# Two of the four weight sums of a seven-product step are formed during the up projection and kept in DRAM

## The chip, the core and the metric

The kernel runs on one core of a Trainium2 chip. TensorE (PE in the profile) multiplies, with its weight loads shown apart as PEld; VectorE is DVE, ScalarE is ACT, GpSimd is POOL, and SyncE (SP) only issues transfers. POOL and ACT can issue transfers too. The metric is device time of one execution in microseconds, as a median of several; lower is better.

## The reference

A decoder layer on 272 positions (16 learned meta tokens and 256 tokens) of width 2048, all in float32:

```
u = rmsnorm(h);  proj = u @ w_in            # retention and mLSTM heads
h = h + concat(ret, hm) @ w_out
u = rmsnorm(h, norm_ffn)
up = causal_dwconv(u @ w_up)                # 2048 -> 2 x 5632, three taps
gate, val = split(up)
h = h + (silu(gate) * val) @ w_down         # 5632 -> 2048
return rmsnorm(h)[16:]
```

The change lies in the last product, with `w_down`, and in the up projection ahead of it.

## The kernel before

**Number format.** Each float32 operand is split into a high part, `hi` (a rounded copy, by ACT, line 128 or 707), and a low part, `lo` (the rest, a subtraction by DVE, line 130 or 709). A product then takes three matmuls: high by high, low by high and high by low. So each 128 x 1024 tile of weights costs one transfer, one ACT cast, one DVE subtraction and its matmuls. Weights arrive in `wraw` (4 buffers) by SP; `whi` and `wlo` have 5 buffers each.

**Up projection.** The 44 blocks of 128 hidden channels are handled in two halves of 22. A block takes two projections (gate and value), each of two half tiles of 24 matmuls on 258 columns (lines 137 to 140). Then `conv3` (line 624) scales the result out of PSUM into `cu` (line 626), applies the taps (lines 628 to 630), and `gt = silu(gt) * vt` (line 721) is the activation. In blocks 2 to 17, DVE also transposes a piece of the residual into `hn` (line 622).

**Down projection.** After each half, the 22 blocks make 11 steps `q` of two blocks, and the 2048 output columns make two pairs `b` = 0 and 2 of two blocks of 512 columns. For a step and a pair there are two forms. A *plain* step loads two weight tiles (`load_step`, line 840) and makes 24 matmuls of 512 columns. A *fast* step (`seven`, line 765) sees step and pair as a 2 x 2 by 2 x 2 block product and makes it by the Strassen-Winograd form with seven products, 21 matmuls. It needs sums of activations (POOL, lines 735 to 738, on the way in the up projection) and four sums of weights: line 773 loads all four weight blocks of the step in one transfer of 1024 KB into `raw`, one of two buffers in dead space of `hT`; DVE forms `ta` (two sums in one operation on 1024 elements, line 776) and `tb` (two dependent sums of 512, lines 777 and 778); then four groups are split into `hi` and `lo` and multiplied. Six steps, `FAST = [1, 2, 4, 5, 7, 8]`, are fast. In the last pair of the second half the last of them, `BOTH`, is made plain, so there are 6 + 6 + 6 + 5 = 23 fast steps.

The four products that serve several outputs are put together in `share` (line 813) after the last fast step of a pair: ACT copies one, DVE makes three sums (lines 819 to 824), and POOL adds four tiles `x` onto `hn` by accumulating transfers (`onto`, line 809). The direct sums `cs` follow at the pair's end.

**The end.** In the last pair the last four plain steps leave out the second column block (`alone`). These products come last: first for rows 0 to 127 (`cs[0, 1]`), then for rows 128 to 255 in two halves of 256 columns. DVE adds them onto `hn` (`add`, line 827), ACT squares and sums (`squares`, line 638), and `finish` (line 652) normalises and stores each row block.

**What sets the order.** A scheduler orders each engine's instructions when the kernel is built, from its own estimate of times; `issue_after` adds an ordering and `high_priority` moves code up. On the chip each engine works in its order and waits on semaphores. SP's and POOL's transfers, too, are issued in order.

## Time and profile before

| | |
|---|---|
| median of 3 executions | 1216.38 us (1215.95, 1216.38, 1219.0) |
| the profiled execution's own time | 1215.93 us |
| its span in the trace | 1214.2 us |
| matmul records | 8965 |
| granted TensorE clock | 0.998 |
| DVE busy | 950.8 us (78%) |
| ACT busy | 704.2 us (58%) |
| POOL busy | 131.0 us (11%) |
| moved by DMA | 236.25 MB, mean 195 GB/s |

The span is the time between the first and the last event in the trace; the execution's own time holds 1.7 us more. Matmuls are pipelined, so a matmul's recorded duration is longer than the distance from its start to the next one's, and it is that distance that counts. An engine's idle time is put down to what ended it. By the trace the up projection of the first half runs from about 470 to 718 us, its down projection to about 835, the second half's up projection to about 1087 and its down projection to the end.

### The profile page before, as it was taken

The numbers are of one execution on the slowest core, as the hardware profiler recorded it, in microseconds if no ns is written. First come the engines' busy times: TensorE is split into PE (matmuls) and PEld (weight loads), VectorE is DVE, ScalarE is ACT, GpSimd is POOL, SyncE is SP. The second block draws the span as 40 slices with busy tenths as digits, with TensorE's granted clock in tenths as the row PEclk, the third lists the DMA queues.
The fourth block names the chain that finished last, engine by engine and source line by source line (L and its number), as shares of the span: only waits on it lengthen the run. The fifth ranks groups of instructions, "written<-read, shape, count | busy, mean of one in ns | idle before, by whom it ended". The sixth has DMA issues, their size and how long they took to land.

```text
span 1214.2 us, 22554 instructions
## 1 busy us (share of the span) xinstructions
PE 1203.5 (99%) x8965; PEld 1156.7 (95%) x8965; DVE 950.8 (78%) x1399; ACT 704.2 (58%) x954; POOL 131.0 (11%) x143
## 2 busy tenths in 40 slices
PE   9999999999999999999999999999999999999997
PEld 9999999999999999999999998888999999998885
DVE  8877778766765767788888789896777777789896
ACT  8647746656556556555555556665555555556564
POOL 0100001111010210010101000202020101100232
PEclk9999999999999999999999999999999999999999
DMA  7764555655564655555555634959655555535946
GB/s 277 267 218 157 167 191 169 201 170 187 183 190 140 208 180 180 182 189 180 186 175 189 247 119 170 263 218 315 229 177 189 177 188 177 188 118 195 274 167 184
DMA packets 74010, 236.25 MB, mean 195 GB/s; under 512 B 13488, under 2 KB 17712, under 8 KB 70832
## 3 DMA queue, kind: packets, MB, share of 16 engines
q1 hardware_dynamic: 68640, 223.85, 55.0%
q0 software_dynamic: 4688, 10.10, 4.1%
q8 instruction: 70, 1.15, 0.4%
q10 hardware_dynamic: 576, 0.85, 0.2%
q14 instruction: 36, 0.29, 0.1%
HBM read 222.98 MB, written 4.46 MB: 187 GB/s over the span
## 4 chain that ended last, share of the span: by engine, by line
PE 96%; DVE 1%; DMA 1%; issue 0%; ACT 0%; SPq 0%; POOL 0%; DVEq 0%; ACTq 0%
PE mmps L137 25%; PE mmps L140 25%; PE mmps L138 25%; PE atps L760 3%; PE atps L761 3%; PE atps L763 3%; PE mmps L795 2%; PE mmps L793 2%; PE mmps L792 2%; PE atps L792 1%; PE atps L795 1%; PE atps L793 1%; PE atps L379 1%; DMA hn<-x 0%; DVE wlo L709 0%; PE atps L371 0%
## 5 line engine op out<-in xcount | busy, mean ns | idle before, releaser
L128 ACT CAST whi<-wraw 128x1024 fp32r<-128x1024 f32 x358 | 375.4, 1050 | 357.9 <-PE mmps L138 250.9
L130 DVE TENSOR_TENSOR wlo<-wraw,whi 128x1024 fp32r<-128x1024 f32 x358 | 441.9, 1237 | 81.3 <-ACT whi L128 74.2
L138 PE MATMUL mmps<-ul,whi 128*128 128x258 f32 x1408 | 345.8, 283 | 0.0
L137 PE MATMUL mmps<-uh,whi 128*128 128x258 f32 x1408 | 345.5, 282 | 0.0
L137 PEld LDWEIGHTS mmps<-uh,whi 128*128 128x128 f32 x1408 | 266.1, 189 | 0.1
L138 PEld LDWEIGHTS mmps<-ul,whi 128*128 128x128 f32 x1408 | 265.1, 188 | 0.1
L137 PE MATMUL mmps<-xh,whi 128*128 128x272 f32 (+2 forms) x864 | 220.1, 287 | 0.0
L138 PE MATMUL mmps<-xl,whi 128*128 128x272 f32 (+2 forms) x864 | 218.8, 286 | 0.0
L140 PE MATMUL mmps<-uh,wlo 128*128 128x258 f32 x1408 | 198.9, 284 | 0.0
L140 PEld LDWEIGHTS mmps<-uh,wlo 128*128 128x128 f32 x1408 | 182.4, 189 | 0.0
L137 PEld LDWEIGHTS mmps<-xh,whi 128*128 128x128 f32 x864 | 162.9, 189 | 0.1
L138 PEld LDWEIGHTS mmps<-xl,whi 128*128 128x128 f32 x864 | 162.5, 188 | 0.0
L140 PE MATMUL mmps<-xh,wlo 128*128 128x272 f32 (+2 forms) x864 | 127.1, 286 | 0.0
L140 PEld LDWEIGHTS mmps<-xh,wlo 128*128 128x128 f32 x864 | 114.7, 188 | 0.0
L626 DVE TENSOR_TENSOR cu<-mmps,rstd 128x258 f32<-128x258 f32 x88 | 37.5, 426 | 78.8 <-PE mmps L140 78.5
L707 ACT CAST whi<-wraw 128x1024 fp32r<-128x1024 f32 x46 | 47.7, 1052 | 37.7 <-DVE wraw L778 22.1
L760 PE MATMUL atps<-whi,mh 128*128 128x512 f32 (+1 forms) x166 | 64.0, 387 | 0.0
L761 PE MATMUL atps<-whi,ml 128*128 128x512 f32 (+1 forms) x166 | 63.8, 386 | 0.0
L138 PE MATMUL mmps<-mixl,whi 128*128 128x258 f32 x256 | 63.1, 283 | 0.0
L137 PE MATMUL mmps<-mixh,whi 128*128 128x258 f32 x256 | 62.5, 283 | 0.0
L709 DVE TENSOR_TENSOR wlo<-wraw,whi 128x1024 fp32r<-128x1024 f32 x46 | 56.5, 1244 | 5.5 <-PE mmps L795 3.0
L707 ACT CAST whi<-hT 128x1024 fp32r<-128x1024 f32 (+1 forms) x46 | 37.4, 836 | 20.6 <-PE atps L793 7.7
(267 smaller groups left out, 1620.2 us busy)
## 6 DMA issues: line engine op xcount, KB each, us to landing
wraw<-in_wu SPq DMA_DIRECT2D x176, 512.0 KB, 3.5
wraw<-in_wi SPq DMA_DIRECT2D x108, 512.0 KB, 4.0
hT<-in_wd SPq DMA_DIRECT2D x23, 1024.0 KB, 5.3
wraw<-in_wd SPq DMA_DIRECT2D x42, 512.0 KB, 5.2
wraw<-in_wo SPq DMA_DIRECT2D x32, 512.0 KB, 3.6
hn<-x POOLq DMA_DIRECT2D x28, 256.0 KB, 6.3
wraw<-in_w SPq DMA_DIRECT2D x7, 320.0 KB, 5.1
hT<-in_xT SPq DMA_DIRECT2D x7, 272.0 KB, 5.5
```

The source lines that it names most:

```text
L128: nc.scalar.copy(hi, raw)
L130: nc.vector.tensor_tensor(out=lo, in0=raw, in1=hi.bitcast(F32), op=ALU.subtract)
L137: nc.tensor.matmul(ps, hi[:, k, :], xh(kk), start=kk == first, stop=False)
L138: nc.tensor.matmul(ps, hi[:, k, :], xl(kk), start=False, stop=False)
L140: nc.tensor.matmul(ps, lo[:, k, :], xh(kk), start=False, stop=kk == last)
L626: nc.vector.tensor_tensor(out=u, in0=ps[:, :NQ], in1=rstd2, op=ALU.mult)
L707: copied = nc.scalar.copy(hi, x)
L709: return copied, nc.vector.tensor_tensor(out=lo, in0=x, in1=hi.bitcast(F32), op=ALU.subtract)
L760: nc.tensor.matmul(ps, ah[i], hi[:, i, cols], start=first and i == 0, stop=False)
L761: nc.tensor.matmul(ps, al[i], hi[:, i, cols], start=False, stop=False)
L763: nc.tensor.matmul(ps, ah[i], lo[:, i, cols], start=False, stop=last and i == 1)
L792: nc.tensor.matmul(o, sh[:, f, m, :], hi[:, i, :], start=begin, stop=False)
```

## The change

A fast step's sums S1 and S3 (the former `ta`) no longer stand in the step. For each fast step and pair, an `Early` object loads three of the four weight blocks (768 KB) during the up projection through POOL's queue, DVE subtracts on 1024 elements, and POOL stores the two sums (512 KB) in DRAM as `kept`. The load is held back by `pace`, a POOL addition of one column of the newest activation `gt`. In the first half twelve of the 14 use one buffer, `x4[:, 1:4]`, one every three projections, and the last two the buffers in `hT`; in the second half 12 take turns in three buffers.

In the down projection a fast step makes three loads by SP instead of one: 512 KB into `wraw`, 512 KB of `kept`, and 256 KB of the remaining block, 1280 KB in all. DVE makes two sums of 512 elements there, into the single buffer `t24`, where it made one of 1024 and two of 512.

Seven steps, `[1, 2, 3, 5, 6, 7, 8]`, are fast; two of them, 7 and 8, are plain in the last pair. That makes 7 + 7 + 7 + 5 = 26 fast steps. The last pair's order is `[0, 1, 4, 2, 7, 3, 5, 6, 8, 9, 10]`, so three half steps follow its `share` where two did. Its `share` is moved up by `high_priority`, and one of its four sums is added by DVE instead of by a transfer. Some constants move into a pool that is given back after attention, `ssq` moves into `hn`, and four `x` tiles become one tile `x4`.

```diff
-    ones = consts.tile([P, P], F32, name="ones")
+    ones = pa.tile([P, P], F32, name="ones")
...
-    ssq = up.tile([P, NQ], F32, name="ssq")
+    ssq = hn[:, 0, 0:NQ]
...
+    x4 = midp.tile([P, 4, 512], F32, name="x4")
...
-    FAST = [1, 2, 4, 5, 7, 8]
+    FAST = [1, 2, 3, 5, 6, 7, 8]
...
+    class Early:
+        def __init__(self, b, q, buf):
+            self.buf = buf
+            self.kept = dram.tile([P, 2, 512], F32, name=f"kept{b}_{q % NQD}", bufs=1)
+            nc.gpsimd.dma_start(buf, io["wd7"][b // 2, q][:, 0:3, :])
+        def finish(self):
+            v = self.buf[:, 1:3, :]
+            nc.vector.tensor_tensor(out=v, in0=v, in1=self.buf[:, 0:1, :].to_broadcast([P, 2, 512]), op=ALU.subtract)
+            nc.gpsimd.dma_start(self.kept, v)
...
+        if half == 0:
+            begins = [2 + 3 * i for i in range(12)] + [37, 38, 40, 41][: len(units) - 12]
+        else:
+            begins = [2 + 39 * i // (len(units) - 1) for i in range(len(units))]
...
+                if running:
+                    running.pop().finish()
+                if 2 * jj + s in begins:
...
+                    reached = gt and nc.gpsimd.tensor_tensor(out=pace, in0=gt[:, 0:1], in1=gt[:, 0:1], op=ALU.add)
+                    with tc.issue_after(reached.ins) if gt else nullcontext():
+                        running.append(Early(b, half * NQD + q, homes[n]))
...
-            nc.sync.dma_start(raw, io["wd7"][b // 2, half * NQD + q])
-            nc.vector.tensor_tensor(out=ta, in0=raw[:, 1:3, :], in1=raw[:, 0:1, :].to_broadcast([P, 2, 512]), op=ALU.subtract)
...
+            nc.sync.dma_start(raw0, io["wd"][b, half * NQD + q])
+            nc.sync.dma_start(raw1[:, 1:3, :], early[b, q])
+            nc.sync.dma_start(raw1[:, 0, :], io["wd"][b + 1, half * NQD + q][:, 1, :])
+            nc.vector.tensor_tensor(out=t24[:, 0, :], in0=raw1[:, 0, :], in1=raw1[:, 1, :], op=ALU.add)
+            nc.vector.tensor_tensor(out=t24[:, 1, :], in0=raw0[:, 1, :], in1=t24[:, 0, :], op=ALU.subtract)
...
-            onto(0, b + 1, x6)
+            if final:
+                nc.vector.tensor_tensor(out=block(0, b + 1), in0=block(0, b + 1), in1=x6, op=ALU.add)
+            else:
+                onto(0, b + 1, x6)
...
-            steps = [0, 1, 3, 2, 6, 4, BOTH, 5, 7, 9, 10] if final else range(NQD)
+            steps = [0, 1, 4, 2, 7, 3, 5, 6, 8, 9, 10] if final else range(NQD)
```

Where an early subtraction stands among DVE's instructions: the first one, in the second block of the first half's up projection, from the end of block 0's activation on. `wlo` are the low parts of the half tiles to come, `ml` that of the activation, and `cu` and `gt` belong to `conv3`. Before:

```order
L721 TENSOR_TENSOR gt<-gt,vt 128x256
L130 TENSOR_TENSOR wlo<-wraw,whi 128x1024
L709 TENSOR_TENSOR ml<-gt,mh 128x256
L626 TENSOR_TENSOR cu<-mmps,rstd_84 128x258
L130 TENSOR_TENSOR wlo<-wraw,whi 128x1024
L630 SCALAR_TENSOR_TENSOR gt<-cu,par,gt 128x256 x2
L130 TENSOR_TENSOR wlo<-wraw,whi 128x1024
```

And now (line numbers of the changed kernel; `x_5817` is `x4`):

```order
L762 TENSOR_TENSOR gt<-gt,vt 128x256
L123 TENSOR_TENSOR wlo<-wraw,whi 128x1024
L739 TENSOR_TENSOR ml<-gt,mh 128x256
L632 TENSOR_TENSOR cu<-mmps,rstd_78 128x258
L123 TENSOR_TENSOR wlo<-wraw,whi 128x1024
L636 SCALAR_TENSOR_TENSOR gt<-cu,par,gt 128x256
L715 TENSOR_TENSOR x_5817<-x_5817 128x1024
L636 SCALAR_TENSOR_TENSOR gt<-cu,par,gt 128x256
L123 TENSOR_TENSOR wlo<-wraw,whi 128x1024
```

Five instructions of DVE lie between the activation on which `pace` waits (L762) and the subtraction that needs the load (L715); everything behind L715 on DVE waits with it.

DVE at the end of the program, from the last sum of `share` on. `hn<-atps,hn` adds a finished PSUM tile onto the result, `rest` and `frt` belong to the normalisation, and `hn<-hn,frt` scales the result's row block. Before:

```order
L824 TENSOR_TENSOR x_13801<-x_13800,mmps 128x512
L130 TENSOR_TENSOR wlo<-wraw,whi 128x1024
...
L829 TENSOR_TENSOR hn<-atps,hn 128x512
L649 TENSOR_REDUCE rest<-ss_5817 128x1
...
L829 TENSOR_TENSOR hn<-atps,hn 128x512
L657 TENSOR_SCALAR frt<-ss_5817,rest 128x1
L829 TENSOR_TENSOR hn<-atps,hn 128x256
...
L669 TENSOR_SCALAR hn<-hn,frt 128x256
L669 TENSOR_SCALAR hn<-hn,frt 128x768
L667 SCALAR_TENSOR_TENSOR hn<-hn,frt,gfin 128x512
L650 TENSOR_SCALAR rest<-rest 128x1
L829 TENSOR_TENSOR hn<-atps,hn 128x256
```

And now:

```order
L870 TENSOR_TENSOR x_5817<-x_5817,mmps 128x512
L123 TENSOR_TENSOR wlo<-wraw,whi 128x1024
L867 TENSOR_TENSOR hn<-hn,x_5817 128x512
L875 TENSOR_TENSOR hn<-atps,hn 128x512 x3
...
L875 TENSOR_TENSOR hn<-atps,hn 128x512
L663 TENSOR_SCALAR frt<-ss_5816,rest 128x1
...
L675 TENSOR_SCALAR hn<-hn,frt 128x256
L675 TENSOR_SCALAR hn<-hn,frt 128x768
L673 SCALAR_TENSOR_TENSOR hn<-hn,frt,gfin 128x512
L875 TENSOR_TENSOR hn<-atps,hn 128x256
...
L656 TENSOR_SCALAR rest<-rest 128x1
L875 TENSOR_TENSOR hn<-atps,hn 128x256
```

The add of DVE in place of a transfer (L867) is new, and the first of the two 256-column adds has moved from ahead of the scaling of rows 0 to 127 to behind it. TensorE's order there has changed as well: the last 512-column products of `cs[0, 1]`, which stood among the 256-column ones, now stand ahead of all 48 of those.

More of the change, by code (lines that the diff above doesn't have):

```diff
@@ L615, in trunk, with x_tile @@
     ss4 = midp.tile([P, 2, 5], F32, name="ss4")
+    x4 = midp.tile([P, 4, 512], F32, name="x4")
+    pace = midp.tile([P, 1], F32, name="pace")
+    def x_tile(i):
+        return x4[:, i, :]
     def transposed_h(i, a):
@@ L703, in trunk @@
         sl = midp.tile([P, len(FAST), 7, P], F32R, name="sl")
-        a21 = [midp.tile([P, P], F32R, name=n) for n in ("a21h", "a21l")]
+        a21 = [midp.tile([P, len(BOTH), P], F32R, name=n) for n in ("a21h", "a21l")]
         def split(hi, lo, x, after=None):
@@ L731, in trunk @@
                 e11, e21, e12, e22 = even[:, 0:P], even[:, P:], gt[:, 0:P], gt[:, P:]
-                if half == 1 and q == BOTH:
-                    split(*a21, e21)
+                if half == 1 and q in BOTH:
+                    split(*(a[:, BOTH.index(q), :] for a in a21), e21)
                 sums = x_tile(0).rearrange("p (a t) -> p a t", a=4)
@@ L800, in seven @@
                         squares(*g)
-                reached = nc.gpsimd.tensor_tensor(out=junk[:, 0:1], in0=tb[:, 1, 0:1], in1=tb[:, 1, 0:1], op=ALU.add)
+                reached = nc.gpsimd.tensor_tensor(out=junk[:, 0:1], in0=t24[:, 1, 0:1], in1=t24[:, 1, 0:1], op=ALU.add)
                 with tc.issue_after(reached.ins):
@@ L853, in trunk @@
             final = half == 1 and b == 2
-            steps = [0, 1, 3, 2, 6, 4, BOTH, 5, 7, 9, 10] if final else range(NQD)
-            fast = [q for q in steps if q in FAST and not (final and q == BOTH)]
+            steps = [0, 1, 4, 2, 7, 3, 5, 6, 8, 9, 10] if final else range(NQD)
+            fast = [q for q in steps if q in FAST and not (final and q in BOTH)]
             plain = [q for q in steps if q not in fast]
@@ L864, in trunk @@
                     if q == fast[-1]:
-                        share(ps, b)
+                        with tc.high_priority() if final else nullcontext():
+                            share(ps, b, final)
                     continue
```

49 lines of the change are left out of this document (28 added, 21 removed).

## The prediction

> **What bounds the kernel now.** I first asked what TensorE waits for (the waits of PE alone, complete):
>
> ```profile
> PE atps L199 <- DVE ones L108: 1.1, 1, 1.1
> PE atps L137 <- ACT whi L224: 0.6, 1, 0.6
> ```
>
> Both are at the program's start; from then on the profile shows no wait of PE. Then the stages by windows: the two up projections, and 100 us out of each down projection. The columns are length, then busy time and number of instructions of PE, PEld, DVE, ACT and POOL, the granted clock, the DMA share and GB/s.
>
> ```profile
> 470.00:718.00 248.00, 248.00 (x2063) 247.94 (x2061) 205.82 (x303) 134.75 (x181) 22.91 (x24) 1.00 0.55 182
> 730.00:830.00 100.00, 100.00 (x431) 80.42 (x430) 91.93 (x98) 59.47 (x66) 10.58 (x12) 1.00 0.71 234
> 837.00:1085.00 248.00, 248.00 (x2064) 248.00 (x2063) 186.21 (x269) 135.78 (x182) 24.74 (x26) 1.00 0.58 187
> 1090.00:1190.00 100.00, 100.00 (x431) 80.43 (x430) 91.52 (x95) 62.83 (x76) 22.00 (x18) 1.00 0.68 218
> ```
>
> Both up projections run at the same 120 ns per matmul (248 / 2063 and 248 / 2064), both down projections at 232 ns (100 / 431). That the numbers are equal while DVE's load differs (206 against 186 us) says that PE sets the pace, not its feeders. DVE has 42 us free in the first up projection, 62 in the second, but only 8 of 100 in the down projections. How far the feeders are ahead in the up projection is read from ACT's longest wait:
>
> ```profile
> ACT whi L128 <- PE mmps L138: 250.9, 200, 4.2
> ```
>
> The casts wait for PE to give back one of the five `whi` buffers, so they stand about four half tiles ahead: 4 x 24 matmuls x 0.120 = 11.5 us, an estimate. So only two things can gain: fewer matmuls, and the end, where PE is not the last.
>
> **Matmuls.** 26 fast steps for 23, each 21 matmuls for 24: nine matmuls fewer, 9 x 0.232 = **-2.1 us**, all on the path. The Trainium skill (TensorE: Matmul & The Clock Gate, section "Wait — 56ns, not 53.3ns?") puts the distance at N / 2.4 GHz plus 2.5 ns, 215.8 ns for 512 columns; by it the nine would be worth 1.9 us. The windows at a clock of 1.00 disagree (232 ns), and the measurement decides.
>
> **DVE in the down projection.** The groups that change:
>
> ```profile
> L130 DVE TENSOR_TENSOR wlo<-wraw,whi 128x1024 fp32r<-128x1024 f32 x358 | 441.9, 1237 | 81.3 <-ACT whi L128 74.2 <-PE atps L795 2.8
> L776 DVE TENSOR_TENSOR wraw<-hT 128x1024 f32<-128x1024 f32 x23 | 29.1, 1265 | 0.1
> L778 DVE TENSOR_TENSOR wraw<-hT,wraw 128x512 f32<-128x512 f32 x23 | 15.7, 683 | 0.1
> ```
>
> A fast step costs DVE 1.27 + 2 x 0.68 for sums (line 777 taken as 778), 3 x 1.24 for three low parts of 1024 and 0.68 (as line 778) for one of 512: 7.0 us against 21 x 0.232 = 4.9 us of PE. Without `ta` it is 5.8. A plain step costs 2 x 1.24 = 2.5 against 5.6. A pair of six fast and five plain steps: DVE 54.4, PE 57.1. With seven and four: DVE 50.5, PE 56.4 (with `ta` left in it would be 59, over PE). So PE stays the bound and DVE gains room; the longest run of fast steps grows from two to four, in which DVE falls back 4 x 0.9 = 3.6 us, where two in a row now cost 4.2. I take 0.
>
> **The early sums.** They add to the first up projection 14 x 1.27 = 18 us of DVE out of 42 free, to the second 12 x 1.27 = 15 out of 62. Each can also make DVE wait for its load. DVE's own work between the activation that `pace` waits for and the subtraction is, for the first one, by the order: 1.24 + 0.42 + 0.43 + 1.24 + 0.48 = 3.8 us (five rows; the last three kinds below), and up to 7.1 where transposes lie between; over the first 14 I count 5.5 in the mean.
>
> ```profile
> L709 DVE TENSOR_TENSOR ml<-gt,mh 128x256 fp32r<-128x256 f32 x20 | 8.4, 418 | 0.0
> L626 DVE TENSOR_TENSOR cu<-mmps,rstd 128x258 f32<-128x258 f32 x88 | 37.5, 426 | 78.8 <-PE mmps L140 78.5
> L630 DVE SCALAR_TENSOR_TENSOR gt<-cu,par,gt 128x256 f32<-128x256 f32 x88 | 42.4, 481 | 1.4
> L735 POOL TENSOR_TENSOR x<-gt 128x128 f32<-128x128 f32 x12 | 5.5, 461 | 119.7 <-DVE gt L721 119.7
> ```
>
> The trace has no 768 KB load through POOL's queue; the nearest are
>
> ```profile
> hT<-in_wd SPq DMA_DIRECT2D x23, 1024.0 KB, 5.3
> hn<-x POOLq DMA_DIRECT2D x28, 256.0 KB, 6.3
> e<-in_decay POOLq DMA_DIRECT2D x8, 209.0 KB, 3.1
> gfin<-in_gfin POOLq DMA_DIRECT2D x1, 1024.0 KB, 5.4
> ```
>
> Between 3.1 us for 209 KB and 5.4 for 1024 KB, nearer the latter: 4.7, with `pace` at 0.5 as L735 (it too starts when `gt` is ready): 5.2 us. So DVE waits up to 1.4 us each time, 14 x 1.4 = 20 us at most, less than the 24 us left, and 11.5 us of lead stand in front of PE. Behind the waiting subtraction on DVE are `conv3` and low parts, on POOL the store and then the activation sums (L776 to L779 of the change), which ACT needs for its next casts; the lead covers these too. Cost taken: 0; it pays only from a mean wait of (24 + 11.5) / 14 = 2.5 us.
>
> **Transfers.** In the first up projection 14 x 1.31 MB in 248 us is 74 GB/s on top of 182; in a fast step 1.31 MB per 4.9 us is 268 GB/s. The DMA engines have shown more:
>
> ```profile
> 785.00:790.00 5.00, 5.00 (x23) 4.05 (x22) 3.82 (x5) 2.30 (x4) 0.00 (x0) 1.00 1.00 381
> DMA to landing us min/median/max: 4.6/5.3/8.7
> ```
>
> The second row is for the 1024 KB weight loads of the fast steps (line 773). Their two buffers remain. A buffer is free after the second of four groups, and is needed two fast steps later: 12 + 21 matmuls x 0.232 = 7.7 us, over the median but under the worst; casts and low parts stand up to four groups, 21 matmuls or 4.9 us, ahead, less 2.3 for one cast and one low part. A landing costs PE only from 7.7 + 2.6 = 10.3 us. Cost taken: 0; not below, since PE has no wait here to lose.
>
> **The end.** Here PE is not last. DVE, PE and ACT:
>
> ```profile
> 1187.85 0.39 PE L795 MATMUL atps<-wlo,sh 128*128 128x512 f32 x1
> 1200.00 0.63 PE L763 MATMUL atps<-wlo,mh 128*128 128x512 f32 x2
> 1204.76 0.40 PE L763 MATMUL atps<-wlo,mh 128*128 128x256 f32 x2
> ...
> 1200.78 0.69 DVE L829 TENSOR_TENSOR hn<-atps,hn 128x512 f32<-128x512 f32 x1 [1.65 <-DMA hn<-x]
> 1201.45 0.68 DVE L829 TENSOR_TENSOR hn<-atps,hn 128x512 f32<-128x512 f32 x1
> 1203.11 0.41 DVE L829 TENSOR_TENSOR hn<-atps,hn 128x256 f32<-128x256 f32 x1
> 1205.48 0.74 DVE L667 SCALAR_TENSOR_TENSOR hn<-hn,frt,gfin 128x512 f32<-128x512 f32 x1
> 1206.21 0.41 DVE L829 TENSOR_TENSOR hn<-atps,hn 128x256 f32<-128x256 f32 x1
> ...
> 1203.56 0.42 ACT L640 ACTIVATE junk<-hn 128x256 f32<-128x256 f32 x1
> 1203.88 0.19 ACT L640 ACTIVATION_READ_ACCUMULATOR junk<-hn 128x1 f32 x1
> ```
>
> PE ends at 1205.16 (E), the last add starts at 1206.21, E + 1.05, and all after it is as before. That add is late since rows 0 to 127 are scaled first, a chain of 4.76 us (1201.45 to the end of L667), and that began late since an add waited for `share`'s last transfer until 1200.78. Now `share` follows PE's last seven-product matmul with 18.7 us of matmuls behind it (56 of 512 columns, 48 of 256 at 0.118) where it had 16.9, and POOL issues three transfers, not four, so the transfer lands about E - 6.3. The last 512-column products are done at E - 5.5. The fourth add then starts at E - 5.5, the chain ends at E - 0.75, but the add of 0.41, a square (0.42 + 0.19) and two small sums now stand behind it, about 1.4 us with gaps: last add at E + 0.65, a gain of 0.4. Bounds: if it starts as PE ends, 1.0 gained; if the transfer lands no earlier than now (E - 4.4), the add comes at E + 2.4, 1.35 lost. I take **-0.4**, by the rows of this same chain.
>
> **At no cost.** `ones` is set third instead of first: the warm-up matmuls are ahead of the first real data, at most 0.25 us. `ssq` in `hn`, the joined `x4`, the moved constants and one more split of `a21` change no work on PE's path.
>
> **Sum.** 1215.93 - 2.1 - 0.4 = 1213.4 for the profiled execution; the median is 0.45 above it, so I forecast 1213.9.
>
> **Rivals.** *Slower: DVE waits for early loads.* With landings like the worst above, 8.7 us, plus 0.5, against 5.5 of own work, 14 waits of 3.7 are 52 us; less 24 free and 11.5 lead leaves 16 us of PE idle in the first up projection, none in the second. Time 1230. It decides from a mean wait of 2.5 us. A late `pace` would do the same; one row shows that it can be:
>
> ```profile
> 1168.84 5.80 POOL L801 TENSOR_TENSOR junk<-wraw 128x1 f32<-128x1 f32 x1 [5.15 <-DVE wlo L709]
> ```
>
> A one-column addition took 5.8 us while DVE worked on end; against it stand twelve of L735 at 0.46. The Trainium skill (SBUF — State Buffer, section "Who interferes with whom") says that a DVE instruction with two SBUF inputs and a GpSimd instruction that reads SBUF exclude each other for a whole instruction; the 5.8 us agree. DVE, once it waits at the subtraction, lets `pace` through. Chance 0.08.
>
> *Late refills in the down projection.* Landings of 12 us in the two places where accumulating transfers run beside fast steps cost 1.7 each, two per place: 6.8 less 2.5 gives 1220.7; with one place, 1217.3. For: the DMA share of 0.71 rises by a quarter. Chance 0.1.
>
> *The end gives nothing.* The matmuls are saved, the chain at the end is no earlier or its bound of +1.35 holds: 1214.3 to 1215.6. Chance 0.12.
>
> *More than the sum.* The end at its other bound, 1.0, and a median as low as the lowest run (1215.95): 1212.85; beyond it only a cost of 512-column matmuls that I don't see. Chance 0.14.
>
> **Numbers.** The forecast's own case (1213.2 to 1214.9) has 0.56. Range: its tail bounds, the end that gives nothing, one place of late refills and half of "more": 1212.2 to 1217.5; outside are the slower rival, two places of refills, and gains that no row shows. A difference of 0.3%, 3.65 us, is about what a measurement of this kernel can tell from none: faster means under 1212.7, slower over 1220.0. Faster 0.15, slower 0.11 (the slower rival and a third of the refills), same 0.74.
>
> **What would show it.** Right: PE's waits again only at the start, nine matmuls fewer at 232 ns in the down projections; a wait for the new DMA ahead of the early subtraction under 1.5 us; the add that waited for `hn<-x` free of it, and the last add within 0.7 us of PE's end. Wrong: PE waiting for low parts of `wlo` in an up projection (early loads), or for casts of `hT` in a down projection (refills), or a last add more than 1.05 us behind PE.

## The result, and the profile after

The changed kernel takes 1234.22 us (median of 5, 1232.6 to 1237.7) where the kernel before takes 1216.38: a ratio of 1.0145, 95% interval 1.0125 to 1.0166. It is slower by 18 us, outside the range I gave. The profiled execution has a span of 1233.8 us.

First the waits of PE, complete, as I read them first before:

```profile
PE atps L801 <- ACT x L925: 7.7, 2, 4.0
PE mmps L133 <- DVE wlo L123: 6.4, 3, 2.3
PE mmps L834 <- ACT whi L737: 3.0, 3, 1.4
PE atps L199 <- DVE ones L173: 1.2, 1, 1.2
PE atps L130 <- ACT whi L224: 0.5, 1, 0.5
```

PE had waited for nothing after the start; now it waits 17 us, for three things: low parts in an up projection (L133), casts of `hT` in a down projection (L834), and, twice for 4 us, ACT's copies of the finished sums `cs` at a pair's end (L801). The windows place them (columns as before):

```profile
470.00:728.00 258.00, 251.57 (x2067) 250.90 (x2067) 207.76 (x308) 127.51 (x178) 49.23 (x70) 0.99 0.72 247
740.00:840.00 100.00, 92.90 (x386) 73.33 (x385) 80.55 (x90) 56.52 (x66) 7.95 (x9) 0.97 0.74 226
852.00:1100.00 248.00, 248.00 (x2059) 248.00 (x2058) 186.05 (x270) 128.74 (x181) 53.56 (x68) 1.00 0.77 258
1110.00:1210.00 100.00, 96.32 (x414) 78.38 (x414) 87.00 (x93) 63.27 (x77) 17.28 (x17) 0.98 0.75 236
```

The second up projection, with 12 early sums, loses next to nothing (0.5 us). The first one and both down projections do, and behind three of the eight stalls (2.31, 4.00 and 3.68 us) PE then runs slowly for some microseconds, which the waits don't count. Windows right behind these three, with a granted clock of 0.76, 0.50 and 0.67:

```profile
642.80:650.00 7.20, 7.20 (x47) 7.20 (x48) 6.13 (x9) 3.19 (x6) 4.04 (x5) 0.76 0.87 283
791.00:796.00 5.00, 4.88 (x12) 3.82 (x13) 2.96 (x3) 4.20 (x8) 1.89 (x3) 0.50 0.97 254
1166.00:1171.00 5.00, 4.86 (x15) 3.88 (x16) 2.96 (x3) 4.72 (x8) 2.10 (x4) 0.67 0.91 250
```

Behind the stalls of 2.21 us (at 617) and 1.91 us (at 716) the granted clock over the next 5 us was 1.00. What the clock takes away in these windows, with the 0.87 of the 5 us from 796 on, adds up to some 6.5 us (an estimate: each window's length times what its clock lacks to 1).

The stages of the main kernels, from the start of a stage's first matmul to that of the next stage's (the last one to its last matmul), from the matmul records of one profiled execution each. Its time and the median over all executions stand behind; where the two are apart, as for `late2` and `six`, the stages are those of an execution longer than most. One execution of `nosub` took 4158 us and is left out. The experiments are told below.

| kernel | up 1 | down 1 | up 2 | down 2 | profiled us | median us |
|---|---|---|---|---|---|---|
| before | 254.5 | 114.8 | 254.1 | 115.5 | 1215.9 | 1216.4 |
| after | 263.8 | 123.4 | 254.6 | 118.3 | 1235.6 | 1234.2 |
| later | 259.6 | 122.7 | 254.6 | 115.3 | 1228.0 | 1229.8 |
| nosub | 255.0 | 120.3 | 254.6 | 116.6 | 1222.1 | 1222.7 |
| late2 | 255.0 | 128.5 | 254.6 | 119.4 | 1233.4 | 1227.3 |
| six | 262.8 | 115.0 | 254.6 | 116.2 | 1225.9 | 1222.7 |
| ord2 | 262.0 | 122.0 | 253.8 | 115.2 | 1229.1 | 1228.4 |
| raw | 255.0 | 120.2 | 254.4 | 119.2 | 1224.8 | 1223.3 |
| late2ord24 | 255.0 | 115.6 | 254.4 | 116.9 | 1219.7 | 1219.7 |
| late36 | 255.0 | 115.3 | 254.6 | 116.2 | 1218.5 | 1217.9 |
| late36ord | 255.0 | 112.9 | 254.4 | 113.5 | 1214.1 | 1213.1 |
| mix2 | 255.0 | 113.8 | 253.9 | 117.9 | 1216.8 | 1218.0 |
| shift_before | 254.5 | 112.6 | 254.1 | 117.6 | 1215.1 | 1216.0 |

So of the 19.6 us between the two spans, 9.3 are the first up projection, 8.6 the first down projection, 2.8 the second and 0.5 the second up projection; what precedes the up projections was 1.2 us shorter in this execution, and what follows the last matmul's start 0.35.

**The first up projection.** Who holds DVE there, after:

```profile
DVE x L715 <- DMA x<-in_wd: 31.6, 8, 6.1
DVE hT L715 <- DMA hT<-in_wd: 3.5, 2, 3.1
```

35.1 us over 14 early subtractions, and the loads land after 6.8 to 7.3 us in the median (4.5 to 9.5 in all):

```profile
x<-in_wd POOLq DMA_DIRECT2D x16, 768.0 KB, 6.8
hT<-in_wd POOLq DMA_DIRECT2D x10, 768.0 KB, 7.3
```

The first stall shows the mechanism, on DVE and then on PE:

```profile
614.25 1.22 DVE L715 TENSOR_TENSOR x<-x 128x1024 f32<-128x1024 f32 x1 [4.18 <-DMA x<-in_wd]
615.39 0.48 DVE L636 SCALAR_TENSOR_TENSOR gt<-cu,par,gt 128x256 f32<-128x256 f32 x1
615.79 1.22 DVE L123 TENSOR_TENSOR wlo<-wraw,whi 128x1024 fp32r<-128x1024 f32 x1
```

```profile
617.06 1.12 PE L133 MATMUL mmps<-uh,wlo 128*128 128x258 f32 x7 [2.21 <-DVE wlo L123]
```

DVE stands 4.18 us at the subtraction, the low part behind it (L123) is late, and PE waits for it.

**A pair's end.** ACT's rows around the copies, after:

```profile
777.13 0.58 ACT L859 COPY x<-mmps 128x512 f32<-128x512 f32 x1
...
790.48 1.07 ACT L925 COPY x<-atps 128x512 f32<-128x512 f32 x2 [4.13 <-DMA hn<-x]
```

The copies empty `cs` for the next pair into the tiles `x4`, which `share` has just filled; they wait until `share`'s transfers from these tiles have landed. DVE's and POOL's rows show when these left:

```profile
779.56 0.68 DVE L861 TENSOR_TENSOR x<-mmps,x 128x512 f32<-128x512 f32 x1
780.16 1.21 DVE L123 TENSOR_TENSOR wlo<-wraw,whi 128x1024 fp32r<-128x1024 f32 x1
781.29 0.68 DVE L862 TENSOR_TENSOR x<-mmps,x 128x512 f32<-128x512 f32 x1
781.89 1.21 DVE L123 TENSOR_TENSOR wlo<-wraw,whi 128x1024 fp32r<-128x1024 f32 x1
783.03 0.68 DVE L864 TENSOR_TENSOR x<-x,mmps 128x512 f32<-128x512 f32 x1
```

```profile
778.02 0.90 POOL L853 DMA_DIRECT2D hn<-x  x1 [62.43 <-ACT x L859]
782.28 0.89 POOL L853 DMA_DIRECT2D hn<-x  x1 [3.36 <-DVE x L862]
784.24 1.77 POOL L853 DMA_DIRECT2D hn<-x  x2 [1.08 <-DVE x L864]
```

Low parts (L123) now stand between `share`'s operations. What ends the first copy's wait, at 790.48, is the landing of the second transfer, the one issued at 782.28: it left 4.26 us after the first and took 8.1 us to land. In the kernel before, DVE's four operations and POOL's rows at the same place were:

```profile
767.70 0.69 DVE L819 TENSOR_TENSOR x<-mmps,x 128x512 f32<-128x512 f32 x1 [0.65 <-PE mmps L795]
768.43 0.69 DVE L820 TENSOR_TENSOR x<-mmps,x 128x512 f32<-128x512 f32 x1
769.15 0.69 DVE L822 TENSOR_TENSOR x<-x,mmps 128x512 f32<-128x512 f32 x1
769.76 0.68 DVE L824 TENSOR_TENSOR x<-x,mmps 128x512 f32<-128x512 f32 x1
```

```profile
766.89 0.93 POOL L811 DMA_DIRECT2D hn<-x  x1 [86.85 <-ACT x L817]
769.43 2.65 POOL L811 DMA_DIRECT2D hn<-x  x3 [1.61 <-DVE x L820]
```

They stood together, all transfers had left 5.2 us after the first began (8.0 us now), and the copies waited for PE alone. The second transfer left 2.54 us after the first and landed after 5.8 us. So at this place the order on DVE accounts for 1.7 us of the delay and the longer landing for 2.3.

**The casts of `hT`.** In a run of fast steps ACT now stands still ahead of its casts. Its row, after:

```profile
L737 ACT CAST whi<-hT 128x1024 fp32r<-128x1024 f32 (+1 forms) x78 | 68.3, 905 | 47.7 <-DVE hT L820 31.8
```

31.8 us in 13 places it waited for L820, DVE's second sum into the single buffer `t24`, which lies in dead space of `hT`. In the kernel before, ACT waited 22.1 us in 8 places for the last sum (L778) too, with DVE busy for 92 of 100 us; now DVE is busy for 81 only (the windows above), and ACT waits longer.

**The end.** The add that had waited for a transfer is free of it, and the last add follows PE at once:

```profile
1224.74 0.40 PE L804 MATMUL atps<-wlo,mh 128*128 128x256 f32 x2
```

```profile
1217.92 1.88 DVE L875 TENSOR_TENSOR hn<-atps,hn 128x512 f32<-128x512 f32 x3
1225.22 0.41 DVE L875 TENSOR_TENSOR hn<-atps,hn 128x256 f32<-128x256 f32 x1
```

PE ends at 1225.14, the last add starts 0.08 us later where it was 1.05, and from PE's end to the span's end it is 8.65 us for 9.00. The two don't match: the last add gained 0.97 us, and what follows it took 0.6 us longer (8.57 us for 7.95).

### The profile page after: what moved, and what is told of

Read it like the earlier page. It is cut to its first block, busy times and chain, and to the rows that moved or that the text cites. A ratio compares the mean times of both kernels' runs of the same rounds, so it can differ in the third digit from the quotient of the medians.

```text
span 1233.8 us, 22843 instructions
## 1 busy us (share of the span) xinstructions
PE 1206.3 (98%) x8956; PEld 1159.0 (94%) x8956; DVE 953.2 (77%) x1418; ACT 697.2 (57%) x963; POOL 179.4 (15%) x228
## 4 chain that ended last, share of the span: by engine, by line
PE 71%; DVE 10%; DMA 10%; issue 5%; POOL 2%; ACT 2%; DVEq 0%; SPq 0%; ACTq 0%; POOLq 0%
PE mmps L130 19%; PE mmps L131 19%; PE mmps L133 18%; DMA x<-in_wd 5%; DVE wlo L123 3%; PE atps L801 2%; PE atps L802 2%; PE atps L804 2%; PE mmps L834 1%; PE mmps L835 1%; DMA hn<-x 1%; PE mmps L837 1%; DVE vt L636 1%; PE atps L835 1%; DVE wlo L739 1%
## 5 line engine op out<-in xcount | busy, mean ns | idle before, releaser
L123 DVE TENSOR_TENSOR wlo<-wraw,whi 128x1024 fp32r<-128x1024 f32 x352 | 433.0, 1232 | 67.2 <-ACT whi L121 65.7
L121 ACT CAST whi<-wraw 128x1024 fp32r<-128x1024 f32 x352 | 364.9, 1045 | 184.9 <-PE mmps L131 132.5
L133 PE MATMUL mmps<-uh,wlo 128*128 128x258 f32 x1408 | 199.5, 284 | 6.4 <-DVE wlo L123 6.4
L133 PEld LDWEIGHTS mmps<-uh,wlo 128*128 128x128 f32 x1408 | 181.4, 189 | 7.0 <-DVE wlo L123 7.0
L133 PE MATMUL mmps<-xh,wlo 128*128 128x272 f32 (+2 forms) x864 | 126.7, 285 | 0.0
L133 PEld LDWEIGHTS mmps<-xh,wlo 128*128 128x128 f32 x864 | 114.2, 188 | 0.0
L739 DVE TENSOR_TENSOR wlo<-hT,whi 128x1024 fp32r<-128x1024 f32 (+1 forms) x78 | 80.1, 1042 | 26.8 <-ACT whi L737 24.0
L737 ACT CAST whi<-hT 128x1024 fp32r<-128x1024 f32 (+1 forms) x78 | 68.3, 905 | 47.7 <-DVE hT L820 31.8
L761 ACT ACTIVATE gt<-gt 128x256 f32<-128x256 f32 x44 | 18.4, 418 | 107.1 <-DVE gt L636 107.0
L801 PE MATMUL atps<-whi,mh 128*128 128x512 f32 (+1 forms) x132 | 52.7, 401 | 7.7 <-ACT x L925 7.7
L715 DVE TENSOR_TENSOR x<-x 128x1024 f32<-128x1024 f32 x16 | 19.6, 1225 | 43.2 <-DMA x<-in_wd 43.2
L853 POOL DMA_DIRECT2D hn<-x x27 | 23.8, 1029 | 197.6 <-ACT x L859 151.4
```

Of the source, the lines that this page charges most:

```text
L121: nc.scalar.copy(hi, raw)
L123: nc.vector.tensor_tensor(out=lo, in0=raw, in1=hi.bitcast(F32), op=ALU.subtract)
L133: nc.tensor.matmul(ps, lo[:, k, :], xh(kk), start=False, stop=kk == last)
L737: copied = nc.scalar.copy(hi, x)
L739: return copied, nc.vector.tensor_tensor(out=lo, in0=x, in1=hi.bitcast(F32), op=ALU.subtract)
L801: nc.tensor.matmul(ps, ah[i], hi[:, i, cols], start=first and i == 0, stop=False)
```

## The experiments

Theory A: DVE stands at the early subtractions until the loads have landed, and PE loses its lead by that. Rivals: POOL's order holds the activation sums (B), or the added transfers slow the weight loads (C). For the pairs' ends, theory D: four fast steps in a row leave DVE, and with it `share`, behind; rival E: the transfers themselves are late. All were timed in rounds with the kernel before (1215.7 to 1216.6 there), except `small`, one execution.

### The first up projection

**later.** The subtraction one projection further back in the code.

```diff
-                if running:
-                    running.pop().finish()
+                if running and 2 * jj + s >= running[0].begun + 2:
+                    running.pop(0).finish()
```

> Each early subtraction is put two projections behind its load where it was one. Theory A (DVE stands at the subtraction until the 768 KB load has landed, and what TensorE loses in the first up projection, some 9 us, is that): the two rows of DVE's wait for these loads (43.2 and 27.3 us) fall under 10 us together, TensorE's 6.4 us of waits for low parts in the first up projection go, and the time falls by 9 at least, to 1225; if the small waits of the first down projection are the same lost lead, to about 1220. Rival B (GpSimd's order: the activation sums and so ACT's casts stand behind the store that waits for the subtraction): the store now waits longer, so TensorE's waits stay or grow, 1234 or more. Rival C (the additional transfers slow the weight loads): nothing changes, 1234.

1229.8 us, ratio 1.0111 [1.0085, 1.0137]. The edit missed: the scheduler left the subtractions nearly where they were, and DVE's waits fell only from 35.1 to 30.8 us. The stage lost 4.2 us less, the waits were 4.3 us less: in this pair of executions a microsecond of wait cost PE one.

**nosub.** The subtraction left out, all transfers and POOL's waits kept.

```diff
-            nc.vector.tensor_tensor(out=v, in0=v, in1=self.buf[:, 0:1, :].to_broadcast([P, 2, 512]), op=ALU.subtract)
```

> The early subtractions are left out; GpSimd stores what was loaded, so DVE never waits for these loads, while all transfers and GpSimd's waiting stay. This leaves the sums S1 and S3 out of the computation. Theory A (DVE's wait): TensorE's waits in the first up projection go, 1225 or, with the lead that is then kept into the down projection, 1220. Rival B (GpSimd's order): GpSimd's store then waits for the load by itself, some 7 us, with the activation sums behind it, so TensorE still waits 6 us there, 1234. Rival C (transfers): 1234.

1222.7 us, 1.0053 [1.0036, 1.0070]. The first up projection takes 255.0 us, and the two small waits near 747 and 773 us are gone too; POOL waited 65.1 us for loads into x4 there, to no harm. B and C fall for this stage. But the subtractions' own work went with their waits.

**late2.** The work stays: the subtraction is put behind the last tap of its block's value projection, and in the first half x4 is loaded every four projections instead of three.

```diff
+            with tc.issue_after(tap.ins):
                 nc.vector.tensor_tensor(out=v, in0=v, in1=self.buf[:, 0:1, :].to_broadcast([P, 2, 512]), op=ALU.subtract)
...
-            begins = [2 + 3 * i for i in range(12)] + [37, 38, 40, 41][: len(units) - 12]
+            begins = [2 + 4 * i for i in range(9)] + [36, 37, 38, 40, 42]
```

> The earlier edit had left the early subtractions where they were among DVE's instructions (waits of 28.9 and 1.9 us in the first up projection after it, 31.6 and 3.5 without it). Now each stands behind the last tap of the same block's value projection, so some 8 us of DVE's own work lie between the activation that starts the load and the subtraction, and in the first half the loads into x4 come one every four projections instead of three. The subtractions keep their own 1.23 us each. Theory A (only the wait counts): DVE's wait for the loads falls under 6 us there and the first up projection takes within 1 us of before, where the changed kernel took 9.3 longer; the two small waits near 747 and 773 us go too: 1223 to 1225. Rival F (the subtractions' 17 us of work are too much for DVE by themselves): half of the loss or more stays, 1229.

Who DVE waits for in the first up projection with it, the rows of the loads:

```profile
DVE x L719 <- DMA x<-in_wd: 1.2, 1, 1.2
DVE hT L719 <- DMA hT<-in_wd: 1.0, 1, 1.0
```

The stage takes 255.0 us with all 14 subtractions in it: theory A holds, the work fits and the wait was the loss. The whole, 1227.3 us (1.0093 [1.0076, 1.0110]), is above what I expected. In the profiled execution, the slowest of five, part of that is my own edit: the load at the 40th projection used the first `hT` buffer a second time, so the first fast step's load waited 9.2 us for its store and PE 4.0 for a cast. `late2ord24` has the same second use; there the store landed after 4.0 us instead of 9.3, and PE had no wait at that place. The later versions (`late3`) load x4 there. And the small waits near 747 and 773 us, which I expected to go, stayed, at 0.4 and 1.4 us.

**small.** Loads of 256 KB, nothing subtracted.

> The early loads are 256 KB instead of 768 and nothing is subtracted (GpSimd stores the loaded block twice; S1 and S3 are left out of the computation). Only the landing is of interest: 6.3 us in the middle and 9.2 at most for 768 KB without the subtractions. If the time is the bytes, shared with the weight loads, it falls to about 4 us (the 209 KB of the kernel before took 3.1); if it is GpSimd's queue itself, it stays above 5.5.

```profile
x<-in_wd POOLq DMA_DIRECT2D x16, 256.0 KB, 4.2
hT<-in_wd POOLq DMA_DIRECT2D x10, 256.0 KB, 4.7
```

A third of the bytes lands after 4.2 to 4.7 us, 768 KB without subtractions after 6.2 to 6.6: it is the bytes, by these medians about 2 us per 512 KB beside the weight loads, on some 3.4 (an estimate).

### The pairs' ends

**six.** Six fast steps as before, early sums kept.

```diff
-    FAST = [1, 2, 3, 5, 6, 7, 8]
+    FAST = [1, 2, 4, 5, 7, 8]
```

> Six fast steps as before, two in a row at most, with early sums kept: 23 fast steps, 9 matmuls more (+2.1 us). Theory D (four fast steps in a row leave DVE behind, so the sums of share and their transfers are late, and the ACT copies that need those tiles hold TensorE 4 us at each pair's end): TensorE's 7.7 us of waits for the copies go with the slower clock behind them, about -10; the first up projection still loses 7 to 9 us with 12 early loads for 14: 1225. Rival E (the transfers themselves are slower now, or the joined tile x4 orders them): the two waits of 4 us stay, 1235.

1222.66 us, 1.0047 [1.0030, 1.0064]: 11.6 better for nine matmuls more. The waits for copies fall from 7.7 to 3.9 us, in four of about 1 us, and do not go. D is half right at best.

**ord2.** `share`'s operations stand together: the low parts of the third and fourth plain tile behind `share` are ordered after its last one.

```diff
-        nc.vector.tensor_tensor(out=lo, in0=raw, in1=hi.bitcast(F32), op=ALU.subtract)
+        with tc.issue_after(hold.ins) if hold else nullcontext():
+            nc.vector.tensor_tensor(out=lo, in0=raw, in1=hi.bitcast(F32), op=ALU.subtract)
...
+                    if summed and not final:
+                        hold, since = summed if since >= 2 else None, since + 1
```

> In the pairs that are not last, DVE's four operations of share stand together, ahead of the low parts of the third plain tile; now two low parts stand between them. Theory D: the third and fourth transfer are issued about 3 us earlier, so the wait for the copies falls from 4.0 to about 1 us at both places, with less of the slow clock behind it: 1226 to 1228, the first up projection unchanged. Rival E (the transfers' landing of about 8 us is what is late): the waits fall by under 1 us each, 1232 or more. If the delayed low parts are late instead, TensorE waits for these, up to 2.7 us at each place.

1228.44 us, 1.0095 [1.0080, 1.0110]: 5.8 better, waits for copies 4.3 us for 7.7. Less than D wanted, more than E allowed; the rows above, where order and landing shared the delay, fit both.

**xc1.** One tile more, and the copies take the tiles in the order of `share`'s transfers.

```diff
-            x6, x7, x5, x1 = (x_tile(i) for i in range(4))
+            x6, x1, x7, x5 = (x_tile(i) for i in range(4))
...
-                        x = x_tile(2 * j + n)
+                        x = x_tile(2 * j + n) if j or n else xc
```

> At the end of a pair that is not last, the first ACT copy goes into a tile of its own and the second into the tile whose transfer was issued first, so neither waits for the later transfers of share; the order on DVE and the four fast steps in a row stay. If the two waits of 4 us are the reuse of the tiles whose transfers land late, TensorE's 7.7 us of waits for the copies fall under 2 us, with 3 us of slow clock behind them: 1224 to 1226. If the copies are late for another reason (ACT's own queue), nothing changes, 1234.

1233.38 us, 1.0135 [1.0120, 1.0151]. A miss: the first two copies no longer wait, the third and fourth do, 7.0 us in all. To pass the wait on does not help.

**late36.** Six fast steps with the repaired loads (the edits of `late2` and `six`).

> Early sums with repaired loads (subtraction behind the last tap, loads one every four projections), but six fast steps of eleven as in the kernel before: 23 fast steps, no matmul saved. If the density of seven is what is left, this one is within 1.5 us of the kernel before, 1215 to 1217, with no wait of TensorE over 1 us. If the early sums' own transfers cost (1280 KB a fast step for 1024, stores and loads more), it stays 3 us or more above it, 1219.

1217.93 us, 1.0017 [1.0008, 1.0026], above the 1215 to 1217 that I expected, with 4.2 us of waits for copies, though at most two fast steps stand in a row. DVE's rows there:

```profile
769.36 0.68 DVE L866 TENSOR_TENSOR x<-mmps,x 128x512 f32<-128x512 f32 x1
771.33 0.69 DVE L824 TENSOR_TENSOR hT<-wraw,hT 128x512 f32<-128x512 f32 x1 [1.29 <-DMA wraw<-in_wd]
771.94 1.22 DVE L123 TENSOR_TENSOR wlo<-wraw,whi 128x1024 fp32r<-128x1024 f32 x1
773.08 0.68 DVE L868 TENSOR_TENSOR x<-x,mmps 128x512 f32<-128x512 f32 x1
```

`share`'s third sum (L868) stands behind a sum of the next pair's fast step (L824), which itself waits for a load.

**late36ord.** The same, with the order of `ord2` and nothing else.

> Six fast steps, early sums with repaired loads, and share's four operations together on DVE in the pairs that are not last. If their order on DVE is what delays the copies, TensorE's 4.2 us of waits for them fall under 1 us and the time comes down by 2 to 3 us, to 1215 to 1216, level with the kernel before. If the transfers themselves are slower beside 1280 KB of loads a step, the waits stay over 2.5 us: 1217 to 1218.

```profile
769.56 0.68 DVE L876 TENSOR_TENSOR x<-x,mmps 128x512 f32<-128x512 f32 x1
770.15 4.62 DVE L125 TENSOR_TENSOR wlo<-wraw,whi 128x1024 fp32r<-128x1024 f32 x4
```

```profile
PE atps L201 <- DVE ones L175: 1.2, 1, 1.2
PE atps L132 <- ACT whi L226: 1.1, 1, 1.1
```

1213.11 us (11 executions, 1212.7 to 1214.1), ratio 0.9975 [0.9967, 0.9984]: no wait of PE after the start, and faster than both kernels. So at six fast steps it is the order on DVE that delays the copies. It is better than I expected by 2 us; part of why is under `shift_before`.

### Seven of eleven

**t24w.** t24 from the weight buffers, for each step its own.

```diff
+            t24 = wpool.tile([P, 2, 512], F32, name="wraw", bufs=4)
             nc.sync.dma_start(raw0, io["wd"][b, half * NQD + q])
```

> The two sums t24 are kept in a buffer of wraw for each step, as the sums were before, instead of one buffer that each step must wait to reuse. If the single buffer makes the small waits for casts of hT (3.0 us of TensorE, near 747, 773 and 837 us), these three go, 1230; if they are DVE's lag behind four fast steps in a row and the lost lead, they stay, 1234; a third load buffer taken from the weights could also bring new waits for wraw.

1236.7 us, 1.0175 [1.0149, 1.0202]: the waits for casts of `hT` fall from 3.0 to 1.3, those near 748, 774 and 839 us are gone, and others, for low parts of `hT` (2.8) and casts of weights (1.6), take their place.

**raw.** No early sums, each step as before, 26 fast steps.

> The 26 fast steps, their order, share and the end stay, but nothing is formed early: each step loads all four blocks in one transfer and DVE forms all sums there, 7.0 us a step against TensorE's 4.9. By the prediction's sums a pair of seven fast and four plain steps then costs DVE 59 us against 56.4 of TensorE: the up projections take what they took before, the down projections lose 2.6 us a pair in three pairs beside the waits for the copies at the pairs' ends, which grow: 1216.4 - 2.1 + 7.8 + 8 or more, 1230. If instead it comes out under 1222, the early sums cost more than they save even with the wait for their loads counted out.

1223.27 us, 1.0059 [1.0044, 1.0074]. Without early sums seven of eleven lose 7.6 us against the kernel before, less than I expected. DVE is busy for 95 of the 100 us from 730 on (92 before), but 4.0 us of PE's waits are for copies, so not all of it is DVE's work. Placed as in the change, the early sums cost 11 us against this; the repaired versions below are 3 to 5 us faster than it, of which some belongs to `share`'s order, which `raw` doesn't have.

**late2ord24**, **late3ord** and **all**: the repairs added up; `all` also gives the copies two tiles that t24 left.

> The three repairs together: subtractions behind the last tap and loads spaced, share's operations of DVE together, t24 in wraw. If the causes are these three and add up, 9 us come back in the first up projection, 5 to 6 at the pairs' ends and 3 to 4 at the small waits: 1215 to 1218. If the waits for the copies are mostly the transfers' landing, 1220 to 1222.

> Subtractions behind the last tap, loads spaced without the second use of the first hT buffer (which had held SP 9.2 us and TensorE 4 us at the first down projection's start), share's operations of DVE together; t24 stays one buffer, and the tiles of share are reused as before. If the lost lead made the small waits, those near 747 and 773 us are gone and the one near 837 us at most is left; the waits for the copies 4 to 5 us together: 1219 to 1220, as with t24 in wraw. If the single t24 matters by itself, 1222 or more.

> All repairs: subtractions behind the last tap, loads spaced, share's operations of DVE together, t24 in wraw, and the two tiles that this frees taken by the first two copies at the pair's end. If the waits found so far are the whole loss, TensorE waits nowhere after the start, the nine matmuls and the end's 0.4 us remain as a gain: 1213 to 1214.5, against 1215.7 to 1216.4 for the kernel before. If it stays above 1216, a cost is left that the waits do not show.

1219.69 (1.0031 [1.0018, 1.0044]), 1220.12 (1.0038 [1.0024, 1.0052]) and 1220.09 (1.0033 [1.0020, 1.0045]). 14 of the 18 us are back. `late3ord` answers what the small waits are; PE's, without those at the start:

```profile
PE mmps L840 <- ACT whi L743: 3.0, 3, 1.4
PE atps L807 <- ACT x L936: 2.8, 3, 1.1
```

Its first up projection takes 255.0 us, so no lead is lost there, and the casts of `hT` still cost 3.0 us. ACT waits 34.7 us for the second sum into `t24`, its single buffer; in `late2ord24`, with a buffer for each step, it waits 6.6, and PE for no cast. The loads near the stage's start differ too between these two, but `t24w`, which differs from the changed kernel in `t24` alone, says the same: no such wait of ACT for 31.8 us. So the single buffer makes these waits. That the last, `all`, is no better than the first, with no wait for copies left at all, is a miss: PE waits for low parts and casts in the second pairs instead, and from PE's end to the span's end it is 10.5 us where the changed kernel took 8.65, since `share`'s last transfer is late there again.

**mix**, **late3ordxc** and **mix2**: t24 outside the weight buffers in the last pair, or copies as in `xc1`; in `mix2` only its last three fast steps.

> As with all repairs, but in the last pair t24 is one buffer outside the weight buffers, as in the changed kernel. With t24 in the weight buffers everywhere the last pair and the end took 117.3 and 12.0 us where the changed kernel's own end took 10.1 and the kernel before 115.5 and 10.4. If the weight buffers held back there by t24 are the cause, about 2.5 us come back: 1216 to 1218. If it is DVE's lag in seven of eleven, nothing changes: 1220.

> Repaired loads, share's operations of DVE together, the copies' tiles taken in the order of the transfers with one tile more, t24 one buffer. Before this edit TensorE still waited 2.8 us for the copies and 3.0 for casts of hT. If the copies' waits are now gone, 1217 to 1218; if they only move on to the third and fourth copy, as they did in the changed kernel with this edit alone, 1220.

> All repairs; t24 is outside the weight buffers only in the last three fast steps of the last pair, so that its first use no longer meets the copies' transfers (a wait of 3.1 us with slow clock behind it, 5.1 in all, in the version before this one). If that wait was an artefact of the edit and nothing else is left, 1213 to 1215, under the kernel before for the first time. If DVE's lag in seven of eleven brings another wait in its place, 1217 to 1219.

1218.86 (1.0025 [1.0016, 1.0034]), 1219.87 (1.0036 [1.0022, 1.0050]) and 1218.0 (1.0020 [1.0008, 1.0031]; 12 executions, 1215.7 to 1222.6). `mix` made a wait of its own (3.1 us for t24, whose buffer the copies' transfers still read). With it removed, low parts and casts of plain steps are late in the second pairs. Seven of eleven never came below the kernel before.

### The matmuls' distance

**shift_before.** The kernel before, with the tile `rest` 64 bytes long, so that all behind it in the pool moves by 32 bytes.

```diff
-    rest = midp.tile([P, 2], F32, name="rest")
+    rest = midp.tile([P, 16], F32, name="rest")[:, 0:2]
```

> The kernel before with one tile of 8 bytes made 64, so that mh, ml, sh, sl and a21, TensorE's stationary operands in the down projection, start at a multiple of 64 bytes; every engine's instructions are the same and in the same order. If that alignment sets the distance of the 512-column matmuls, it goes from 233 to 229 ns, about 960 of them give 4 us, and the time is 1212. If the distance is a phase that waits or the order of the instructions set, nothing changes: 1216.

Two windows of it in the down projections:

```profile
730.00:830.00 100.00, 100.00 (x439) 81.96 (x438) 91.89 (x98) 58.24 (x66) 10.56 (x12) 1.00 0.71 234
1090.00:1190.00 100.00, 97.70 (x424) 79.19 (x423) 86.99 (x91) 61.39 (x74) 25.60 (x17) 1.00 0.65 209
```

439 matmuls in 100 us where the kernel before made 431: by the records 229 ns from one to the next for 233 (a window also counts the matmuls that its edges cut), by a shift of addresses alone. But the time is 1215.96 us, ratio 0.9997 [0.9985, 1.0009]: in the second down projection PE, now faster, waits for casts (2.5 us), and what the first gained is lost. So the shift alone, without early sums, brings the first down projection as far as `late36ord` does (112.6 and 112.9 us), and not the second (117.6 and 113.5). `late36ord` has the same 439 in both:

```profile
730.00:830.00 100.00, 100.00 (x439) 82.05 (x438) 84.16 (x90) 61.65 (x67) 10.67 (x12) 1.00 0.79 242
1090.00:1190.00 100.00, 100.00 (x439) 82.05 (x438) 86.84 (x90) 64.73 (x76) 16.86 (x17) 1.00 0.78 248
```

Its DVE has 84 and 87 us to do in 100, where the kernel before has 92. Its two down projections gain 1.9 and 2.0 us (114.8 to 112.9, 115.5 to 113.5), which is more than the 1.9 us between the two spans: all it gains is the shorter distance, which its feeders can follow. That the early sums are what lets them follow is likely by DVE's load, but no run separates it: there is none of the shifted kernel with six fast steps, this order and no early sums.

## Why the prediction was wrong, point by point

- **The early sums, the step that failed.** I put the landing at 4.7 us, from 209 KB in 3.1 and 1024 KB in 5.4, the waits at 20 us "at most", and took their cost at 0; they were 35.1, by landings of about 7, and the stage lost 9.3 us. The 5.4 was a single landing: the same load took 7.8 us in the changed kernel and 5.1 in `nosub`. The rival with 1230 us was this mechanism at its own price (a mean wait of 3.7 us; it was 2.5) and had a chance of 0.08. It should have stood higher: the 8.7 us behind its price stood in a row beside the ones I took mine from.
- **The threshold of 2.5 us failed too.** The mean came out at just 2.5, where I had no loss, and PE lost 9.3. I had set waits against DVE's free time of the whole stage. In order of time: up to the first stall at 614 us there were eight subtractions of 10 us, six of them with waits, 24 us in all, 34 together; free by then were 144 us times 17%, 24, and the lead of 11.5, 36. So the lead was as good as gone there, by these estimates, and what DVE had free later came too late for it.
- **DVE in the down projection.** "I take 0" for four in a row: wrong. I had counted the fast steps but not `share`, whose operations stand apart in DVE's new order, with low parts between them, and with two fast steps in a row too (`late36`). I had looked for `share` only at the program's end. That cost 7.7 us of waits and the slow clock behind them (windows of 0.50 and 0.67). `ord2` gave 5.8 us back; with six fast steps the order alone took all 4.2 us of the waits away (`late36` to `late36ord`).
- **Transfers, and a term left out.** Late refills were not the loss: the casts of `hT` cost 3.0 us, but ACT waited there for DVE's sum into `t24`, not for a load. I had given that single buffer no term. Two of the three waits went with the early subtractions (`nosub`), which looked like lead missing from the up projection; `late3ord`, which loses no lead there, has three such waits again. What the buffer costs in time is open: without it (`t24w`, `late2ord24`) these waits went and others came.
- **Matmuls.** Nine fewer are there, 8965 to 8956. That 512 columns take 232 ns was a property of the kernel before, not of the matmul: away from stalls it is 229 in the changed kernel (233 before, from the records), about 960 times 4 ns, up to 4 us that I did not see and that the stalls hid. The 215.8 ns of the Trainium skill (TensorE: Matmul & The Clock Gate, "Wait — 56ns, not 53.3ns?") lie under both.
- **The end.** The gain of 0.35 us and the last add within 0.7 us of PE's end came as predicted, the size in part by luck: the add gained 0.97 us for the 0.4 predicted, and what follows it lost 0.6, which I had at nothing. Nor does it hold in every repaired version: in `all` and `late36ord` an add waits for the transfer again, the last add starts 1.98 and 1.45 us behind PE's end, and the end is longer than in the kernel before.
- **A late `pace`** did not come: 0.18 to 1.24 us, 0.67 in the median, against the 5.8 of one row before; with that, the rule of the Trainium skill (SBUF — State Buffer, "Who interferes with whom") on two-input DVE operations and GpSimd decided nothing here.

What stays open: why seven of eleven, with all these repairs, still loses 2 to 4 us (in `mix2` PE still waits 3.5 us behind the start) and varies by 7 us from one execution to the next (`mix2`); and what sets the matmuls' distance (only one shift, of all tiles behind `rest` together, was tried, and in `xc1`, below, it changed with no shift).

## What to carry to other kernels

An instruction that waits for a transfer on a busy in-order engine must stand behind more of that engine's own work than the transfer's longest landing; set its waits against the free time in order of time, not over the stage. Whatever hands buffers back between two stages (here `share`) has to stand together on its engine: look at its place in the new order even where the change doesn't name it. And a moved loop may want only half of a change: six fast steps with early sums and the repaired order came out 3 us below the kernel before, and the seventh step, at its best (`mix2`), 5 us above that.

## What the runs showed of the hardware that I had not expected

Matmuls of 512 columns with a weight load each have more than one steady distance at a granted clock of 1.00. In the records of the kernel before, starts follow each other by 231, 232 and 237 ns again and again, 700 ns for three; in the other kernels, nearly everywhere, by 226, 229 and 232, 687 ns for three. A shift of tiles by 32 bytes moved the kernel before to the second pattern, and in `xc1` the distance changed to 233 ns within the last pair, right after a stall of 3.5 us at 1170, with no change of addresses (87 matmuls in 20 us for 89):

```profile
1125.00:1145.00 20.00, 20.00 (x89) 16.41 (x88) 18.77 (x21) 13.11 (x16) 0.00 (x0) 1.00 0.80 258
1175.00:1195.00 20.00, 20.00 (x87) 16.19 (x86) 18.65 (x20) 12.76 (x17) 3.85 (x4) 1.00 0.79 255
```

And a stall can cost more than itself: in the 5 us after 791 us, behind the longest one, PE made 12 matmuls where 22 would fit, 2.3 us more, at a granted clock of 0.50. A stall of 2.31 us was followed by a slow clock (0.76 over 7.2 us), one of 2.21 us in the same execution was not (1.00).
